# A two-layer decoder trunk on one Trainium2 core: product order, copy placement and stream splits around the Strassen stage and the first stick-breaking group

## The chip, the cores and the metric

One core of a Trainium2 chip. The metric is device time in microseconds of one execution, the median of several runs; lower is better. The engines are TensorE (PE), VectorE (DVE), ScalarE (ACT), GpSimd (POOL) and SyncE (SP), which here issues the DMAs.

## The reference, cut to what matters

512 tokens of width 2048 pass through two layers. Layer 0 is sparse attention with an indexer (top 128 keys of a query), layer 1 is stick-breaking attention over keys and values that are computed once from the stream. Each layer ends in a projection, a LayerNorm over `ALPHA * x + h`, and a gated per-layer embedding.

```python
def mixer_b(x, w_in, w_o, k, v):
    q, gate = jnp.split(x @ w_in, [WIDTH_B], axis=-1)
    ...
        z = jnp.einsum('bqngd,bsnd->bngqs', qg, k) * (HEAD_DIM ** -0.5)
        strict = key_pos[None, :] < t[:, None]
        log_om = jnp.where(strict, -jax.nn.softplus(z), 0.0)
        suffix = lax.cumsum(log_om, axis=log_om.ndim - 1, reverse=True) - log_om
        a = jnp.where(strict, jnp.exp(jax.nn.log_sigmoid(z) + suffix), 0.0)
        o = jnp.einsum('bngqs,bsnd->bqngd', a, v)
    ...
    return (o * jax.nn.silu(gate)) @ w_o

for i in range(DEPTH):                       # DEPTH = 2, layer 0 uses mixer_a
    h = mixer(x)
    x = layer_norm(ALPHA * x + h, ln_g[i], ln_b[i])
    x = x + (p[i] @ w_ple[i]) * jax.nn.sigmoid(x @ w_ple_gate[i])
```

16 heads of 128 in four groups that share keys and values; all arrays are float32.

## The kernel before, in words

**Precision.** Every float32 operand is split in two: `split` copies it to a rounded high part on ScalarE (`ACTIVATE`, line 111 in the profile, the common helper) and subtracts it on VectorE for the low part. `mm3` (lines 134 to 136) then makes a product of three matmuls: high by high, high by low, low by high. A product of a 128-row weight block with 512 columns is three matmuls of 512 columns.

**Weights.** They come through `next_raw`: 512 KB loads on SP's queue into three `raw` buffers, in the order of the list `units`, which also holds blocks of the stream `x` and, in layer 1, the two halves of `x2` that have to come back from DRAM. `plain_items` and `strassen_items` split them into `wh` and `wl` (three buffers each); `Ahead` keeps two blocks split ahead of the one in use.

**Order.** TensorE's order is the program's. On the other engines a planner may move an instruction forward when it is ready, unless it is pinned: `keep_in_program_order` sets it behind the instruction traced last on its engine (which may itself have been moved forward). `Paced` pins everything while `pinned[0]` is set. Small pieces of work wait in the queue `bg`; `pumped` issues one of them, pinned, after every n-th product, `drain` the rest. `interleave` spreads the products of one generator between the steps of another.

**Start.** `first_items` brings, for each pair k2 of 128-row blocks, a stream unit and two weight units (`iq` and `k`). It splits the stream blocks (`xh`, `xl`) and the weights.

**Strassen.** The value projection and the four query projections of layer 1 are five chunks of Strassen's method (Winograd's form) with seven products over 256 token columns. `gemm_s` runs k over eight steps of two weight blocks j, that is 14 products a step. `strassen_items` makes the weight sums `s1` to `s4` in `st` (four VectorE additions a step) and splits them into `sh` and `sl`. The seven sums build up in seven of the eight PSUM banks; `product_banks` shifts the banks by one from chunk to chunk, so that product i of a chunk uses the bank in which product i-1 of the chunk before was left. In `gemm_s`, the first step (k=0) fetches both weight blocks and issues products 0 to 2 of both and then 3 to 6 of both; all later steps go block by block. `combine` reads the banks into four quarters: three copies by ScalarE (`u`, `c21`, `c12`), two VectorE additions, three more in `rest`, and three `onto` additions that go to `bg`.

**Stick-breaking.** Four groups g of four heads, ten units u = (i, kb) each, by the generator `sticks`: `logits` (product `z`, then Abs, Exp, Ln on ScalarE, a VectorE operation, a GpSimd mask on the diagonal, and the split `sh`, `sl`), `weights` (two or four matmuls with triangular matrices onto `z`, Exp, split), `values` (product `o`). Between their steps stand the products of that group's gate projection (16 weight blocks of four products). For group 0, `gate_first` takes the blocks 8 to 15 first, since blocks 0 to 7 have to be restored: the right half of `xh` and `xl` held Strassen sums, and `restore` splits the returned halves of `x2` into them. `split_keys`, `split_scaled` and `split_values` make the split keys, scaled queries and values. The first 20 gate products of group 0 run alone, with those splits in `bg`; then `px`, a pool that holds the work tiles of the sticks, is opened where the value tiles were.

**Last part.** `finish_layer` does projection, LayerNorm and embedding, once a layer; it is not changed.

Of the kernel before, what the change touches and what calls it, by code (L numbers as in the profile page):

```python
# [18 lines left out]
T = 512  # L19
# [58 lines left out]
def trunk_kernel(  # L78
# [79 lines left out]
    def plain(kb):  # L158
        return XH[kb], XL[kb]
# [159 lines left out]
    bg = deque()  # L319

    def paced(fn, *args):
        pinned[0] = True
        fn(*args)
        pinned[0] = False

    def one():
        paced(bg.popleft())
# [8 lines left out]
    def drain():  # L336
        while bg:
            one()
# [42 lines left out]
    def gemm_s(items, C3, M):  # L381

        rows = M[0].shape[1]
        for k in range(NK // 2):
            b11, t1 = ((XH[k][:, s], XL[k][:, s]) for s in (slice(0, H), slice(H, T)))
            b21, b22 = ((XH[k + 8][:, s], XL[k + 8][:, s]) for s in (slice(0, H), slice(H, T)))
            t2, t3, t4 = ((C3[k][0][:, i], C3[k][1][:, i]) for i in range(3))
            sides = (b11, b21, t2, t3, t1, b22, t4)
            terms = []
            for j in range(rows):  # L390
                pinned[0] = k == j == 0
                a11, a22, a12, s1, s2, s3, s4 = next(items)
                pinned[0] = False
                terms.append((a11, a12, s2, s3, s1, s4, a22))
                if k:
                    order = [(i, j) for i in range(7)]
                elif j == rows - 1:

                    order = [(i, n) for some in (range(3), range(3, 7)) for n in range(rows) for i in some]
                else:  # L400
                    continue
                for i, n in order:
                    first, final = (n == 0, n == 1) if rows == 2 else (i % 2 == 0, i % 2 == 1 or i == 6)
                    mm3(M[i][:, n], terms[n][i], sides[i], k == 0 and first, k == NK // 2 - 1 and final)
                    yield

    def quarter(x, i, j0=0, rows=2):
# [5 lines left out]
    def combine(wp, M, dst):  # L413

        m1, m2, m6, m7, m5, m3, m4 = M
        u = wp.tile([128, 2, H], F32, name="u", tag="u", bufs=1)[:, : m1.shape[1]]
        c11, c22, c12, c21 = (dst(i) for i in range(4))
        pinned[0] = True
        act.activation(u, m1, AF.Copy)
        act.activation(c21, m7, AF.Copy)  # L420
        act.activation(c12, m5, AF.Copy)
        dve.tensor_tensor(c11, m2, u, ALU.add)
        dve.tensor_tensor(u, m6, u, ALU.add)
        pinned[0] = False
# [10 lines left out]
        return [lambda c=c: onto(c) for c in (c12, c21, c22)]  # L435

    def build_plain(k):
        for n in (k, k + 8):
# [76 lines left out]
    for g in range(4):  # L515
        add_job(w_in_b, g * 512, strassen=True)
    x2 = dram.tile([D, T], F32, name="x2")
    for k in (4, 5, 6, None, 7, None, 0, 1, 2, 3):
        if k is None:
            first = 4 * (units[-1][1] == 14)  # L520
# [590 lines left out]
    finish_layer(0, xT, x2, (pk_, pv_), first_sums, first_blocks)  # L1111


    with ps_:
        sp = ps_.enter_context(tc.tile_pool(name="sp1", bufs=1))
        C3.extend(c3_tiles(sp, range(4, 8)))
# [14 lines left out]
        for n, dst in enumerate((Vf, *F)):  # L1131
            M = product_banks(4 - n)
            gemm = pumped(gemm_s(items, C3, M), 8)
            if n == 1:
                steps(gemm, 40)
                for t in range(4):
                    steps(gemm, 16)
                    turn_values(t)
            run(gemm)
            drain()  # L1140
            bg.extend(combine(sp, M, lambda i: quarter(dst, i)))
        drain()

    pc_ = ExitStack()
    pc = pc_.enter_context(tc.tile_pool(name="pc", bufs=1))
# [7 lines left out]
    def split_values(t):  # L1153
        split(*V[t], Vf[:, :, t * 128 : (t + 1) * 128])

    def split_scaled(g, i):
        qh, ql = (pc.tile([128, 4, 128], F32R, name=f"q{s}", tag=f"q{s}", bufs=4) for s in "hl")
# [5 lines left out]
    def restore(raw, k):  # L1163
        split(XH[k][:, H:T], XL[k][:, H:T], raw[:, k % 4])

    def gate_items():
        for k, n in ((0, 6), (4, 2)):
            yield from plain_items([(512, n)])
            raw = next_raw()
            bg.extend(lambda raw=raw, k=k: restore(raw, k) for k in range(k, k + 4))  # L1170
        yield from plain_items([(512, 8), *[(512, NK)] * 3])

    items = Ahead(gate_items(), 2)

    def gate_first(banks):

# [14 lines left out]
    pv_.close()  # L1191
    px_ = ExitStack()
    px = px_.enter_context(ss(name="px", bufs=1, side="right"))

    def work():
        return px.tile([128, 512], F32, name="wk", tag="wk", bufs=4)
# [5 lines left out]
    def sticks(g, Q):  # L1202
# [34 lines left out]
        def weights(u):  # L1237
# [6 lines left out]
            act.activation(a, z, AF.Exp)  # L1244
            if kb == i:
                strict(a)
            parts = tuple(px.tile([128, 512], F32R, name=f"a{s}", tag=f"a{s}", bufs=2) for s in "hl")
            split(*parts, a)
            state[u] = parts

# [6 lines left out]
                act.activation(F[g][:, :, i * 128 : (i + 1) * 128], out[i].rearrange("p (h q) -> p h q", h=4), AF.Copy)  # L1257

        for s in range(12):
            for fn, u in ((logits, s), (weights, s - 1), (values, s - 2)):  # L1260
                if s == 1 and fn == weights:
                    for _ in range(4):
                        yield
                if 0 <= u < 10:
                    fn(u)
                    yield

    for g in range(4):
        tc.keep_in_program_order(act.preload_act_table_set("natural_log_exp_and_others"))
        if g:  # L1270
            banks = mm_banks("g")
            gemm = pumped(gemm_w(items, plain, banks))
        if g < 3:
            bg.append(lambda g=g: split_keys(g + 1))
        interleave(sticks(g, Q), 30 + 4, gemm, 52 if g else 40, lead=8 * (g > 0))
        if g < 3:
            for i in range(4):
                split_scaled(g + 1, i)
# [57 lines left out]
```

## Time and profile before

| | us |
|---|---|
| median of 3 runs | 1887.45 (1887.42 to 1887.73) |
| the profiled execution | 1888.32 |
| its span, first to last instruction | 1886.6 |
| TensorE busy | 1873.0 (99%) |
| VectorE busy | 1192.3 (63%) |
| ScalarE busy | 940.0 (50%) |
| Strassen chunks, from about | 1033.7 to 1242.5 |
| stick-breaking, first group, from about | 1242.5 to 1314 |

The granted TensorE clock is 1.00 throughout. DMAs take about a third of the 16 engines' time. In a timeline row stand the start, the duration, the engine, the line, the operation, what it writes and reads, and in brackets how long its engine was idle before it and what ended that; `sh` in Strassen is a weight sum, in the sticks a split of the softplus; `f` and `E` are result tiles.

### The profile page before, as it was taken

To read this page: it belongs to the slowest core of one execution; us is meant where nothing else is said; L and a number is where in the kernel's file an instruction comes from. 1 tells how busy PE (TensorE), PEld (TensorE's weight loads), DVE (VectorE), ACT (ScalarE), POOL (GpSimd) and SP (SyncE) were. 2 spreads that over 40 slices of the span, in tenths; PEclk is the share of its full clock that TensorE was granted. 3 is DMA by queue.
4 is the path that set the end of the run, shared out by engine and by line. 5 is a ranking of instruction groups with operands and counts; after the bars stand their busy time and mean duration, and the time that the engine had idled before them with its cause. 6 is when DMAs were issued, how large, how long until landed. Compare 5 with 4: busy or idle time off the path is not lost.

```text
span 1886.6 us, 25028 instructions
## 1 busy us (share of the span) xinstructions
PE 1873.0 (99%) x9229; PEld 1585.3 (84%) x9229; DVE 1192.3 (63%) x2327; ACT 940.0 (50%) x1714; POOL 26.4 (1%) x46
## 2 busy tenths in 40 slices
PE   9999999999999999999999999999999999999998
PEld 8898888888888888888888999987888888888887
DVE  4768678566555455675368878876655545567534
ACT  3546333456554432474245444468877743347422
POOL 0000000000000000000000000000100000000000
PEclk9999999999999999999999999999999999999999
DMA  5432333322222532423343333331122153242333
GB/s 184 137 115 65 101 91 100 97 60 68 68 68 67 178 101 73 128 91 112 115 139 112 101 102 101 101 112 56 56 67 68 59 187 99 74 129 89 123 101 112
DMA packets 111179, 189.22 MB, mean 100 GB/s; under 512 B 8528, under 2 KB 29008, under 8 KB 111056
## 3 DMA queue, kind: packets, MB, share of 16 engines
q1 hardware_dynamic: 111056, 187.62, 32.5%
q8 instruction: 72, 1.18, 0.3%
q14 instruction: 51, 0.42, 0.1%
HBM read 179.21 MB, written 8.39 MB: 99 GB/s over the span
## 4 chain that ended last, share of the span: by engine, by line
PE 94%; DVE 2%; ACT 1%; DMA 1%; issue 1%; SPq 0%; DVEq 0%; ACTq 0%
PE g L135 12%; PE g L134 12%; PE g L136 12%; PE o L135 7%; PE o L136 7%; PE o L134 7%; PE q L134 3%; PE q L135 3%; PE q L136 3%; PE m L136 3%; PE m L135 3%; PE m L134 3%; PE z L1242 2%; PE k L135 1%; PE k L136 1%; PE k L134 1%
## 5 line engine op out<-in xcount | busy, mean ns | idle before, releaser
L111 ACT ACTIVATE wh<-raw 128x512 fp32r<-128x512 f32 (+3 forms) x685 | 396.2, 580 | 653.0 <-PE g L135 231.9
L111 DVE TENSOR_TENSOR wl<-raw,wh 128x512 fp32r<-128x512 f32 (+3 forms) x685 | 429.4, 629 | 448.9 <-ACT wh L111 430.4
L134 PE MATMUL g<-xh,wh 128*128 128x512 f32 x1024 | 403.9, 394 | 0.2
L135 PE MATMUL g<-xl,wh 128*128 128x512 f32 x1024 | 400.6, 391 | 0.4 <-DVE xl L111 0.4
L136 PE MATMUL g<-xh,wl 128*128 128x512 f32 x1024 | 399.7, 390 | 0.0
L136 PEld LDWEIGHTS g<-xh,wl 128*128 128x128 f32 x1024 | 192.2, 188 | 41.0
L134 PEld LDWEIGHTS g<-xh,wh 128*128 128x128 f32 x1024 | 192.4, 188 | 39.5 <-ACT wk L111 1.1
L135 PEld LDWEIGHTS g<-xl,wh 128*128 128x128 f32 x1024 | 192.4, 188 | 38.8 <-DVE xl L111 1.2
L136 PE MATMUL o<-xh,wl 128*128 128x512 f32 x512 | 199.3, 389 | 0.0
L135 PE MATMUL o<-xl,wh 128*128 128x512 f32 x512 | 199.2, 389 | 0.0
L134 PE MATMUL o<-xh,wh 128*128 128x512 f32 x512 | 199.2, 389 | 0.0
L136 PEld LDWEIGHTS o<-xh,wl 128*128 128x128 f32 x512 | 96.1, 188 | 20.2 <-DVE wl L111 0.3
L135 PEld LDWEIGHTS o<-xl,wh 128*128 128x128 f32 x512 | 96.1, 188 | 20.1
L134 PEld LDWEIGHTS o<-xh,wh 128*128 128x128 f32 x512 | 96.1, 188 | 19.9
L134 PE MATMUL q<-xh,wh 128*128 128x512 f32 x256 | 99.6, 389 | 0.0
L135 PE MATMUL q<-xl,wh 128*128 128x512 f32 x256 | 99.6, 389 | 0.0
L136 PE MATMUL q<-xh,wl 128*128 128x512 f32 x256 | 99.6, 389 | 0.0
L111 ACT ACTIVATE sh<-st 128x512 fp32r<-128x512 f32 x80 | 49.5, 629 | 84.7 <-PE m L135 46.6
L111 DVE TENSOR_TENSOR sl<-st,sh 128x512 fp32r<-128x512 f32 x80 | 54.4, 689 | 41.1 <-ACT sh L111 41.1
L111 DVE TENSOR_TENSOR xl<-f,xh 128x512 fp32r<-128x512 f32 x80 | 54.3, 686 | 11.3 <-ACT f L111 11.0
L111 ACT ACTIVATE wk<-z 128x512 f32<-128x512 f32 x80 | 47.3, 591 | 25.1 <-PE z L136 17.2
L136 PEld LDWEIGHTS q<-xh,wl 128*128 128x128 f32 x256 | 48.1, 188 | 10.0
(286 smaller groups left out, 3345.1 us busy)
## 6 DMA issues: line engine op xcount, KB each, us to landing
raw<-w_in_a SPq DMA_DIRECT2D x95, 512.0 KB, 3.7
raw<-w_in_b SPq DMA_DIRECT2D x64, 512.0 KB, 3.8
raw<-w_ple_gate SPq DMA_DIRECT2D x52, 512.0 KB, 3.7
raw<-w_o_a SPq DMA_DIRECT2D x24, 512.0 KB, 3.7
raw<-w_o_b SPq DMA_DIRECT2D x24, 512.0 KB, 3.7
raw<-w_kv_b SPq DMA_DIRECT2D x16, 512.0 KB, 3.7
raw<-w_ple_gate SPq DMA_DIRECT2D x24, 256.0 KB, 2.9
f<-xT SPq DMA_DIRECT2D x4, 1024.0 KB, 6.5
```

Source lines behind the costliest of these rows:

```text
L111: ins = method(*args, **kw)
L134: pe.matmul(out, a[0], b[0], start=start, stop=False)
L135: pe.matmul(out, a[0], b[1], start=False, stop=False)
L136: pe.matmul(out, a[1], b[0], start=False, stop=stop)
L1242: pe.matmul(z, m, p, start=False, stop=n == len(terms), skip_group_check=True)
```

## The change

What it does, in the order of the diff:

- In `first_items`, the splits of stream blocks are pinned from k2 = 2 on, so they stand behind the weight splits traced before them.
- `paced` restores what `pinned[0]` was.
- `gemm_s` issues all seven products of a weight block before it fetches the next, in k=0 too.
- `combine` copies `m5` to `c22` instead of `c12`, and `rest` reads bank `m3` first. After the last chunk, `combine_last` takes its place: one ScalarE copy and seven VectorE additions, all pinned, nothing in `bg`. Ahead of it the first two gate blocks are split.
- The returned halves of `x2` come after the gate's units 4 to 7 and after unit 0; their restores follow in `bg` when the ninth and the eleventh gate block are fetched, with the queries of i = 3 and the keys of group 1 behind them.
- In group 0 the ScalarE table for Exp and Ln is loaded right after the last chunk. Only the keys and two query blocks are split first; nine gate products, the first logits, one gate product, the second logits, eight gate products beside which two value blocks are split, the first weights, two more gate products with the other value blocks. The rest, 44 gate products, is spread over 27 steps (before: 44 left after the lead of 20, 40 of them over 34 steps), with one piece of `bg` after every second product.
- The work pool `px` lies apart from the values now; only the split weights (`ah`, `al`) go where the values were, and the first unit's use query buffers.
- Of the next group's four query splits, three go to `bg` during the group; before, all four came at its end.

```diff
@@ first_items
-            if k2:
-                for a in range(2):
-                    split(*plain(2 * k2 + a), x[:, a])
+            for n in (2 * k2, 2 * k2 + 1) if k2 else ():
+                was, pinned[0] = pinned[0], k2 > 1
+                split(*plain(n), x[:, n % 2])
+                pinned[0] = was
@@ gemm_s
-                terms.append((a11, a12, s2, s3, s1, s4, a22))
-                if k:
-                    order = [(i, j) for i in range(7)]
-                elif j == rows - 1:
-                    order = [(i, n) for some in (range(3), range(3, 7)) for n in range(rows) for i in some]
-                else:
-                    continue
-                for i, n in order:
...
+                terms = ((a11, b11), (a12, b21), (s2, t2), (s3, t3), (s1, t1), (s4, b22), (a22, t4))
+                for i, (a, b) in enumerate(terms):
...
@@ combine
-        act.activation(c12, m5, AF.Copy)
+        act.activation(c22, m5, AF.Copy)
...
-            dve.tensor_tensor(c22, c12, c21, ALU.add)
-            dve.tensor_tensor(c12, m3, c12, ALU.add)
+            dve.tensor_tensor(c12, m3, c22, ALU.add)
+            dve.tensor_tensor(c22, c22, c21, ALU.add)
             dve.tensor_tensor(c21, c21, m4, ALU.subtract)
...
+    def combine_last(wp, M, dst):
...
+        act.activation(u, m1, AF.Copy)
+        for out, a, b, op in (
+            (c11, m2, u, ALU.add),
+            (u, m6, u, ALU.add),
+            (c21, m7, u, ALU.add),
+            (c22, m5, c21, ALU.add),
+            (c12, m5, u, ALU.add),
+            (c12, m3, c12, ALU.add),
+            (c21, c21, m4, ALU.subtract),
+        ):
+            dve.tensor_tensor(out, a, b, op)
@@ units
-    for k in (4, 5, 6, None, 7, None, 0, 1, 2, 3):
+    for k in (4, 5, 6, 7, None, 0, None, 1, 2, 3):
@@ gate_items
-        for k, n in ((0, 6), (4, 2)):
+        for k, n in ((0, 8), (4, 2)):
             yield from plain_items([(512, n)])
             raw = next_raw()
             bg.extend(lambda raw=raw, k=k: restore(raw, k) for k in range(k, k + 4))
+            bg.append((lambda: split_scaled(0, 3)) if k == 0 else (lambda: split_keys(1)))
-        yield from plain_items([(512, 8), *[(512, NK)] * 3])
+        yield from plain_items([(512, 6), *[(512, NK)] * 3])
@@ group 0
-    bg.append(lambda: split_keys(0))
-    for i in range(4):
-        bg.append(lambda i=i: split_scaled(0, i))
-        bg.append(lambda i=i: split_values(i))
-    banks = mm_banks("g")
-    gemm = pumped(gate_first(banks))
-    steps(gemm, 20)
+    log_exp()
+    bg.append(lambda: split_keys(0))
+    bg.extend(lambda i=i: split_scaled(0, i) for i in range(2))
+    banks = mm_banks("g")
+    chunk = gate_first(banks)
+    gemm = pumped(chunk)
+    steps(gemm, 9)
+    first = sticks(0, Q)
+    steps(first, 1)
+    steps(gemm, 1)
+    steps(first, 1)
+    bg.extend(lambda i=i: split_values(i) for i in range(2))
+    steps(gemm, 8)
+    drain()
+    steps(first, 1)
+    bg.extend(lambda i=i: split_values(i) for i in range(2, 4))
+    steps(gemm, 2)
...
+    bg.append(lambda: split_scaled(0, 2))
+    gemm = pumped(chunk, 2)
...
-        interleave(sticks(g, Q), 30 + 4, gemm, 52 if g else 40, lead=8 * (g > 0))
+        if g:
+            interleave(sticks(g, Q), 30 + 4, gemm, 52, lead=8)
+        else:
+            interleave(first, 30 - 3, gemm, 64 - 20)
```

More of the change, by code (lines that the diff above doesn't have):

```diff
@@ L321, in paced @@
     def paced(fn, *args):
-        pinned[0] = True
+        was, pinned[0] = pinned[0], True
         fn(*args)
-        pinned[0] = False
+        pinned[0] = was
     def one():
@@ L435, in combine @@
         return [lambda c=c: onto(c) for c in (c12, c21, c22)]
+    def combine_last(wp, M, dst):
+        m1, m2, m6, m7, m5, m3, m4 = M
+        u = wp.tile([128, 2, H], F32, name="u", tag="u", bufs=1)
+        c11, c22, c12, c21 = (dst(i) for i in range(4))
+        pinned[0] = True
+        act.activation(u, m1, AF.Copy)
[9 more added lines that the diff above has]
+            dve.tensor_tensor(out, a, b, op)
+        pinned[0] = False
     def build_plain(k):
@@ L517, in trunk_kernel @@
     x2 = dram.tile([D, T], F32, name="x2")
-    for k in (4, 5, 6, None, 7, None, 0, 1, 2, 3):
+    for k in (4, 5, 6, 7, None, 0, None, 1, 2, 3):
         if k is None:
-            first = 4 * (units[-1][1] == 14)
+            first = 4 * (units[-1][1] == 0)
             units.append((x2.rearrange("(k p) t -> p k t", p=128)[:, first : first + 4, H:T],))
@@ L1111, in trunk_kernel, with restore, gate_items @@
     finish_layer(0, xT, x2, (pk_, pv_), first_sums, first_blocks)
+    def restore(raw, k):
+        split(XH[k][:, H:T], XL[k][:, H:T], raw[:, k % 4])
+    def gate_items():
+        for k, n in ((0, 8), (4, 2)):
+            yield from plain_items([(512, n)])
+            raw = next_raw()
+            bg.extend(lambda raw=raw, k=k: restore(raw, k) for k in range(k, k + 4))
+            bg.append((lambda: split_scaled(0, 3)) if k == 0 else (lambda: split_keys(1)))
+        yield from plain_items([(512, 6), *[(512, NK)] * 3])
     with ps_:
@@ L1140, in trunk_kernel @@
             drain()
-            bg.extend(combine(sp, M, lambda i: quarter(dst, i)))
-        drain()
+            if n == 4:
+                items = Ahead(gate_items(), 2).prime()
+                combine_last(sp, M, lambda i: quarter(dst, i))
+            else:
+                bg.extend(combine(sp, M, lambda i: quarter(dst, i)))
     pc_ = ExitStack()
@@ L1246, in weights @@
                 strict(a)
-            parts = tuple(px.tile([128, 512], F32R, name=f"a{s}", tag=f"a{s}", bufs=2) for s in "hl")
+            if u or g:
+                parts = tuple(pa_late[0].tile([128, 512], F32R, name=f"a{s}", tag=f"a{s}", bufs=2) for s in "hl")
+            else:
+                parts = [a.rearrange("p h q -> p (h q)") for a in scaled_parts()]
             split(*parts, a)
@@ L1259, in sticks @@
         for s in range(12):
+            if s > 2 and units[s - 3][1] == 0 and g < 3:
+                bg.append(lambda i=units[s - 3][0]: split_scaled(g + 1, i))
             for fn, u in ((logits, s), (weights, s - 1), (values, s - 2)):
-                if s == 1 and fn == weights:
-                    for _ in range(4):
-                        yield
                 if 0 <= u < 10:
@@ L1266, in sticks @@
                     yield
+                if g and s == 1 and fn == logits:
+                    for _ in range(4):
+                        yield
+    log_exp()
[15 more added lines that the diff above has]
+    steps(gemm, 2)
+    pv_.close()
+    pa_late.append(px_.enter_context(ss(name="pal", bufs=1, side="right")))
+    bg.append(lambda: split_scaled(0, 2))
+    gemm = pumped(chunk, 2)
     for g in range(4):
-        tc.keep_in_program_order(act.preload_act_table_set("natural_log_exp_and_others"))
         if g:
+            log_exp()
             banks = mm_banks("g")
             gemm = pumped(gemm_w(items, plain, banks))
-        if g < 3:
-            bg.append(lambda g=g: split_keys(g + 1))
-        interleave(sticks(g, Q), 30 + 4, gemm, 52 if g else 40, lead=8 * (g > 0))
-        if g < 3:
-            for i in range(4):
-                split_scaled(g + 1, i)
+        if 0 < g < 3:
+            bg.append(lambda g=g: split_keys(g + 1))
+        if g:
+            interleave(sticks(g, Q), 30 + 4, gemm, 52, lead=8)
+        else:
+            interleave(first, 30 - 3, gemm, 64 - 20)
+        drain()
+        if g < 3:
+            split_scaled(g + 1, 3)
         for h in range(4):
```

23 lines of the change are left out of this document (9 added, 14 removed).

## The prediction, as put on record before the run

> **What bounds the kernel now.** I read the page first, then the waits of TensorE (PE), then the timeline around each wait. In the page, busy time by engine:
>
> ```profile
> span 1886.6 us, 25028 instructions
> ...
> PE 1873.0 (99%) x9229; PEld 1585.3 (84%) x9229; DVE 1192.3 (63%) x2327; ACT 940.0 (50%) x1714; POOL 26.4 (1%) x46
> ```
>
> TensorE is idle for 13.6 us of the span. No matmul is added or removed by the change, so it can only win back stalls of TensorE or make new ones. Who ended those stalls is in the view of waits (us in total, times, longest):
>
> ```profile
> PE m L136 <- DVE sl L111: 2.2, 4, 0.6
> PE z L1242 <- ACT sh L111: 1.4, 2, 0.9
> PE spun L156 <- DVE xl L111: 1.4, 1, 1.4
> PE m L136 <- DVE wl L111: 1.2, 4, 0.3
> PE z L1242 <- DVE sl L111: 0.8, 3, 0.3
> PE iq L134 <- ACT wh L111: 0.6, 1, 0.6
> ```
>
> Three places: the Strassen products `m` (3.4 us idle in eight waits), the first stick-breaking group `z` (2.2 in five), one stall in the first projection `iq`. The diff touches all three. Idle time understates a stall, since a matmul's row overlaps its successor; I count lost time between starts.
>
> **Strassen's boundary.** The TensorE timeline where the third of five chunks begins:
>
> ```profile
> 1117.46 0.28 PE L134 MATMUL m<-xh,wh 128*128 128x256 f32 x1
> ...
> 1122.62 0.28 PE L135 MATMUL m<-xl,wh 128*128 128x256 f32 x1
> 1123.12 0.39 PE L136 MATMUL m<-xh,wl 128*128 128x256 f32 x1 [0.21 <-DVE wl L111]
> ...
> 1123.91 0.28 PE L135 MATMUL m<-c3l,sh 128*128 128x256 f32 x1
> 1124.66 0.39 PE L136 MATMUL m<-c3h,sl 128*128 128x256 f32 x1 [0.48 <-DVE sl L111]
> ```
>
> The chunk starts at 1117.46. Its k=0 is 14 products of three matmuls, 42 starts; 1122.62 is the 44th start after it, so a matmul takes 5.16 / 43 = 0.12 and a product 0.36. Then 1122.62 to 1123.12 should be 0.12 and is 0.50, and 1123.91 to 1124.66 is 0.75: lost 0.38 + 0.63 = 1.01 for 0.69 idle. Scaled to the 3.4 idle of the eight waits: 3.4 x 1.01 / 0.69 = 5.0 us over four boundaries. What VectorE does meanwhile:
>
> ```profile
> 1118.05 0.68 DVE L111 TENSOR_TENSOR u<-m,u 128x512 f32<-128x512 f32 x1
> 1118.65 0.68 DVE L111 TENSOR_TENSOR f<-f 128x512 f32<-128x512 f32 x1
> 1119.43 0.69 DVE L111 TENSOR_TENSOR f<-m,f 128x512 f32<-128x512 f32 x1
> 1120.04 0.68 DVE L111 TENSOR_TENSOR f<-f,m 128x512 f32<-128x512 f32 x1
> 1120.64 0.42 DVE L111 TENSOR_TENSOR st<-st,raw 128x256 f32<-128x256 f32 x1
> 1120.97 1.29 DVE L111 TENSOR_TENSOR f<-f,u 128x512 f32<-128x512 f32 x2
> 1122.18 0.42 DVE L111 TENSOR_TENSOR st<-raw,st 128x256 f32<-128x256 f32 x1
> 1122.51 1.49 DVE L111 TENSOR_TENSOR wl<-raw,wh 128x384 fp32r<-128x384 f32 x3
> 1123.92 1.89 DVE L111 TENSOR_TENSOR sl<-st,sh 128x512 fp32r<-128x512 f32 x3
> ```
>
> These are the previous chunk's sums (`u`, three of `rest`), then `s2` of the next weight block, two `onto` additions, only then `s4`, and the copies `wl` and `sl` that TensorE waits for. Before the change both blocks of k=0 are fetched ahead of any product, so an `onto` is pinned only behind the second block's last instruction, which the planner had already floated forward; so two slip in between `s2` and `s4`.
>
> After it, the first block's `s2`, `s4`, `wl`, `sl` are traced, then one product, then the first `onto`, pinned behind that `sl`. The second `onto` can still slip. Step by step: the three `rest` operations stay three, `s2` at 1120.64; `s4` right behind it (1121.0) or behind one `onto` of 0.6 (1121.6); `wl` (1.41 / 3 = 0.47 each) done by 1121.5 to 1122.5; `sh` on ScalarE and then `sl` (0.6 each) done by 1122.6 to 1123.3. TensorE wants `wl` at 1122.74 and `sl` at 1117.46 + 14 x 0.36 + 2 x 0.36 + 0.24 = 1123.46. Both are in time, with 0.2 to spare in the worse case. The `onto`s and the second block come after; it is wanted 2.52 later, and has about 1.9 of VectorE's work ahead of it. So the 5.0 us go.
>
> What is late next is a PSUM bank. Plain order reaches product 4 after 3 products, not 6: at 1117.46 + 1.08 = 1118.54. That bank held `m6`, and its reader `u<-m,u` ends at 1118.73. A wait of 0.19 and some 0.06 of signal: 0.25, four times 1.0 us; bounds 0 (VectorE does it one 0.33 `st` earlier) and 2.0 (one 0.47 copy gets in front, less the slack). The seventh product is at 1119.62; its bank's reader now comes right behind `u`, at 1118.65 + 0.68 = 1119.33, which is why the swap in `rest` matters: left at 1119.43 + 0.69 = 1120.12 it would cost 0.5 each. Net for Strassen: -4.0 (between -5.0 and -3.0).
>
> `combine_last` issues seven VectorE additions and one ScalarE copy for eight and three. The fourth gate bank was emptied by ScalarE and is now emptied by the third VectorE operation; at a boundary's pace it would be free 1.27 + 0.60 = 1.87 after the chunk's end, and is wanted after three gate products of three matmuls of 0.23, 2.04. Nothing lost: the cover is 0.17 at that pace, and if it goes, the cost is that excess, once.
>
> **The first stick group.** TensorE, then ScalarE, GpSimd (POOL), and the table of stretches (length, busy PE, PEld, DVE, ACT, POOL, clock, DMA share, GB/s):
>
> ```profile
> 1262.03 0.39 PE L136 MATMUL g<-xh,wl 128*128 128x512 f32 x1
> 1263.33 0.50 PE L1242 MATMUL z<-sh,tri 128*128 128x512 f32 x1 [0.92 <-ACT sh L111]
> 1264.06 0.50 PE L1242 MATMUL z<-sl,tri 128*128 128x512 f32 x1 [0.23 <-DVE sl L111]
> ```
>
> ```profile
> 1253.92 1.32 ACT L111 ACTIVATE xh<-raw 128x256 fp32r<-128x256 f32 x4
> 1255.26 1.28 ACT L111 ACT_TABLE_LOAD   x1
> ```
>
> ```profile
> 1242.50:1256.10 13.60, 13.60 (x62) 11.27 (x61) 13.44 (x25) 9.91 (x20) 0.00 (x0) 1.00 0.29 83
> 1256.10:1285.00 28.90, 26.67 (x110) 20.13 (x109) 20.07 (x35) 25.92 (x51) 4.20 (x6) 1.00 0.35 108
> ```
>
> A 512-column matmul is 0.23, so 1262.03 to 1263.33 lost 1.07 and the next step 0.50: 1.57 for 1.15 idle. Scaled to 2.2 idle: 3.0 us. The cause is ScalarE, busy 25.92 of 28.90 in the group's first half, and only 9.91 of 13.60 before. The change takes from that half the table load (1.28), the first restored half (1.32), and the chains of the first two logits, and puts them into the emptier stretch or behind.
>
> Now z(0) comes after 9 gate products instead of 20, and weights(0) after gate, z(1) and 8 gate products: 10 x 0.68 = 6.8 after z(0) ends. Before, it was 1 gate, z(1) and 6 gates: 8 x 0.68 = 5.4, and 1.07 late; so 6.5 sufficed even with everything in the way. The later units gain too: 44 gate products now fill 27 steps (1.63 each) where 40 filled 34 (1.18); over four gaps that is 4 x 0.45 x 0.68 = 1.2 us more between a logits and its weights, against waits of at most 0.9. I keep 0.5 as residue, because for some 8 us from weights(0) on ScalarE has values, queries, two weight blocks and restores of 0.3 to 0.6 each in front of two logits. Bounds: 0 and all 3.0. Net -2.5.
>
> What is queued behind the moved steps: the seven pinned sums stand on VectorE ahead of `kl` and `ql`. They end about 4.5 us into the gate, z(0) wants them at 9 x 0.68 = 6.1; two copies of 0.6 fit. On SP's queue the halves of `x2` go behind four weight units; each holds one of three `raw` buffers for 8 gate products. The weight load that waits for it is wanted 9 gate products later, over 6 us, longer where sticks lie between. The restores come 8 gate products (5.4 us) ahead of their first reader, at one restore for every two products. Next groups' queries go one by one into gaps of the old group: same work, no price.
>
> A row speaks against more copies around the diagonal masks:
>
> ```profile
> 1269.81 0.64 POOL L1200 TENSOR_SCALAR_AFFINE_SELECT wk<-wk 128x512 f32<-128x512 f32 x1 [3.84 <-ACT wk L111]
> 1274.74 1.02 POOL L1200 TENSOR_SCALAR_AFFINE_SELECT run<-run 128x512 f32<-128x512 f32 x1 [4.30 <-DVE run L111]
> ```
>
> A select takes 0.64, once 1.02; four lie on logits chains of the group, so 4 x 0.38 = 1.5 is the most this adds to the chains, and the spacing above absorbs it for three. The Trainium skill's "SBUF — State Buffer", section "Who interferes with whom", says that a VectorE instruction with two SBUF inputs and a GpSimd instruction that reads SBUF exclude each other for the whole instruction; by that rule the delay could reach a whole copy, 4 x 0.68 = 2.7, and the group's gain would be 0.3 instead of 2.5. The trace shows 0.38 at the worst select, so I stay with the rows.
>
> **The start.**
>
> ```profile
> 26.48 1.15 ACT L111 ACTIVATE xh<-raw 128x512 fp32r<-128x512 f32 x2 [5.67 <-DMA raw<-xT]
> 27.54 1.65 ACT L111 ACTIVATE wh<-raw 128x512 fp32r<-128x512 f32 x3
> ```
>
> ```profile
> 27.29 0.34 PE L136 MATMUL iq<-xh,wl 128*128 128x384 f32 x1
> 28.20 0.44 PE L134 MATMUL iq<-xh,wh 128*128 128x384 f32 x1 [0.57 <-ACT wh L111]
> 28.48 0.33 PE L135 MATMUL iq<-xl,wh 128*128 128x384 f32 x1
> 29.09 0.45 PE L136 MATMUL iq<-xh,wl 128*128 128x384 f32 x1 [0.28 <-DVE wl L111]
> ```
>
> ScalarE stood 5.67 us before a block of the stream that was still on its way, with a ready weight block behind it. At 0.17 a matmul, 0.74 + 0.44 = 1.2 are lost. Pinned, the stream's splits (k2 from 2) stand behind the weights of the pair before; a pair is about 11 us of matmuls, and the split waits for about a quarter of it, so it still comes several us early. Gain -1.2, bounds 0 and -1.2.
>
> **The sum.** -4.0 - 2.5 - 1.2 = -7.7; two small gaps at the group switches, whose four query copies are now mostly made earlier, may give 0.5 more, of which I take 0.2. -7.9 on the profiled execution's 1888.32 is 1880.4. The median of the three runs is 1887.45, 0.87 below it; there: **1879.6 us**.
>
> **Rivals.** *The copies keep slipping.* VectorE's order is the planner's choice wherever nothing is pinned; the second `onto` and copies of later blocks may still go before `s4`, and the bank wait comes on top. Two slips of 0.6 leave `sl` about 0.5 late, with the bank wait 0.75 of 1.25 kept at each boundary. Strassen then gives 2.0, all together 5.9: 1881.6; with the group's residue at 2 as well, 1883.1. For it: `s4` behind two `onto`s today. Against: the first is now pinned.
>
> *It doesn't do what it says.* What is unpinned floats back to where it was, or each stall gets a successor of its size: 1887.5, 0 to 2 either way.
>
> *Slower: ScalarE bounds the first group.* Today it is 90% busy over half of the group. If the pinned pieces put it behind, TensorE's in-order queue stands at each of ten weights, not five times. At 1.57 a wait that is 15.7, less the 3.0 already there: +12.7, with -4.0 and -1.2 elsewhere +7.5: 1895. It decides when the chain of a unit exceeds the 6.7 us of TensorE's work between a logits and its weights. Against it: the old need of 6.5.
>
> **The numbers.** Forecast 62%, slipping copies 18%, no effect 10%, slower 10%. About 0.2%, 3.8 us, is what a measurement can tell from no change, so faster (below 1883.7) 0.80, same 0.10, slower 0.10. All stalls gone and no bank wait would be 5.0 + 3.0 + 1.2 + 0.5 = 9.7, 1877.7; scaling idle to lost time may be short by a tenth: low end 1876.7. High end: slipping copies and a residue, 1884.0; beyond it lie the last two cases.
>
> **What would show it.** In the waits: no `m <- sl` or `m <- wl`, instead `m <- DVE u` of 0.1 to 0.3 four times; `z <- sh` gone or under 0.5; no `iq` wait near 28. In VectorE's timeline `s4`, `wl`, `sl` ahead of the first `onto`. The table load at about 1241, and ACT's share in the group's first half well under 90%. I am wrong if `m` waits on `f` or still on `sl`, or if the `z` waits grow in number.

## The result, and the profile after

| | before | after |
|---|---|---|
| median, us (lowest to highest of six runs each, same chip) | 1887.52 (1887.41 to 1887.88) | 1880.09 (1879.05 to 1881.19) |
| ratio to before | | 0.9961, interval 0.9948 to 0.9974 |
| the profiled execution, its span | 1888.32, 1886.6 | 1879.05, 1877.2 |

The forecast was 1879.6, range 1876.7 to 1884.0. From the page of the kernel after, span and busy time by engine:

```profile
span 1877.2 us, 25016 instructions
...
PE 1868.1 (100%) x9229; PEld 1586.2 (85%) x9229; DVE 1192.1 (64%) x2326; ACT 939.2 (50%) x1712; POOL 26.5 (1%) x46
```

Span minus busy PE was 13.6 and is 9.1. The span fell by twice that, 9.4, because lost starts and slower matmuls count as busy. TensorE's waits after (total, times, longest):

```profile
PE spun L156 <- DVE xl L111: 1.4, 1, 1.4
PE z L134 <- ACT qh L111: 1.0, 1, 1.0
PE z L1255 <- ACT sh L111: 0.5, 1, 0.5
PE z L135 <- DVE ql L111: 0.4, 1, 0.4
PE g L135 <- DVE xl L111: 0.4, 2, 0.2
PE z L1255 <- DVE sl L111: 0.2, 1, 0.2
```

All eight `m` waits and both `iq` waits are gone from this table; of `z` two smaller ones stay, and waits for `qh` and `ql` are new. To size every loss alike, *lost time* below is the sum, over a stretch, of each matmul's start-to-start time less the median for its shape in the kernel before:

| kernel | start | Strassen | group 0 | groups 1 to 3 | rest | span |
|---|---|---|---|---|---|---|
| before | 1.98 | 5.42 | 4.82 | 3.77 | 9.29 | 1886.6 |
| after | 0.44 | 1.85 | 3.59 | 1.44 | 8.51 | 1877.2 |
| start alone | 0.44 | 5.39 | 4.81 | 3.78 | 8.83 | 1884.6 |
| Strassen alone | 1.54 | 1.84 | 5.30 | 3.76 | 9.19 | 1883.0 |
| sticks alone | 1.90 | 5.40 | 3.62 | 1.46 | 8.80 | 1882.5 |
| after, fourth query first | 0.44 | 1.83 | 2.02 | 2.58 | 9.09 | 1877.3 |
| after, run again | 0.44 | 1.83 | 5.42 | 1.41 | 9.06 | 1879.5 |
| after, old `rest` | 0.44 | 2.83 | 5.36 | 1.42 | 9.50 | 1880.9 |
| before, 32 bytes | 2.25 | 5.37 | 4.41 | 3.82 | 8.68 | 1885.9 |
| before, 96 bytes | 1.94 | 5.41 | 3.92 | 1.15 | 7.35 | 1881.1 |
| after, 32 bytes | 0.44 | 1.80 | 3.82 | 2.23 | 8.14 | 1877.8 |
| after, 96 bytes | 0.44 | 1.84 | 3.53 | 0.74 | 7.52 | 1875.4 |
| combined | 0.44 | 3.43 | 1.29 | 0.72 | 7.68 | 1874.9 |
| 96 bytes and query first | 0.44 | 1.87 | 1.29 | 0.71 | 7.28 | 1872.9 |

(Groups 1 to 3 are the last three stick groups; "rest" is the first 60 matmuls, the middle and the last part.) From before to after the rows give 1.54 + 3.57 + 1.23 + 2.33 + 0.78 = 9.45, the 9.4 of the spans. Two entries are surprises: group 0 gave half of what was forecast, and groups 1 to 3, for which 0.2 was forecast, gave 2.33. The rows below the second belong to the experiments.

**Strassen's boundary after.** TensorE, then VectorE, at the third chunk (the chunk starts at 1114.31):

```profile
1115.27 0.28 PE L136 MATMUL m<-c3h,sl 128*128 128x256 f32 x1
...
1115.63 0.39 PE L134 MATMUL m<-c3h,sh 128*128 128x256 f32 x1
1115.86 0.28 PE L135 MATMUL m<-c3l,sh 128*128 128x256 f32 x1
```

```profile
1114.89 0.68 DVE L111 TENSOR_TENSOR u<-m,u 128x512 f32<-128x512 f32 x1
1115.50 0.68 DVE L111 TENSOR_TENSOR f<-m,f 128x512 f32<-128x512 f32 x1
...
1117.61 0.42 DVE L111 TENSOR_TENSOR st<-st,raw 128x256 f32<-128x256 f32 x1
1117.95 0.68 DVE L111 TENSOR_TENSOR f<-f,u 128x512 f32<-128x512 f32 x1
1118.55 0.42 DVE L111 TENSOR_TENSOR st<-raw,st 128x256 f32<-128x256 f32 x1
1118.88 1.02 DVE L111 TENSOR_TENSOR wl<-raw,wh 128x384 fp32r<-128x384 f32 x2
1119.82 0.68 DVE L111 TENSOR_TENSOR sl<-st,sh 128x512 fp32r<-128x512 f32 x1
1120.42 0.69 DVE L111 TENSOR_TENSOR f<-f,u 128x512 f32<-128x512 f32 x1
```

The fourth product starts at 1115.63, 0.24 late, as its bank is read by `u<-m,u` until 1115.57: the bank wait of the forecast, 0.20 to 0.24 at the four boundaries, with another 0.10 in the step behind it. One `onto` (1117.95) did get between `s2` and `s4`, the worse of the two cases that the prediction allowed; the second now comes after `sl` (1120.42) and not before it.

At the other three boundaries `sl` is still late, by waits too short for the table. VectorE, then TensorE, at the second chunk:

```profile
1077.44 0.69 DVE L111 TENSOR_TENSOR sl<-st,sh 128x512 fp32r<-128x512 f32 x1
```

```profile
1077.95 0.28 PE L135 MATMUL m<-c3l,sh 128*128 128x256 f32 x1
1078.19 0.39 PE L136 MATMUL m<-c3h,sl 128*128 128x256 f32 x1
```

The second matmul starts 0.24 after the first instead of 0.12, and the next step loses another 0.10. So a boundary loses 0.34 in all at the third chunk and 0.51 to 0.52 at the others, where 0.25 was forecast.

**Group 0 after.** TensorE and ScalarE around the new wait:

```profile
1275.80 0.50 PE L134 MATMUL z<-qh,kh 128*128 128x512 f32 x1 [1.01 <-ACT qh L111]
1276.69 0.50 PE L135 MATMUL z<-ql,kh 128*128 128x512 f32 x1 [0.39 <-DVE ql L111]
```

```profile
1267.99 0.63 ACT L111 ACTIVATE wh<-raw 128x512 fp32r<-128x512 f32 x1 [1.02 <-DMA raw<-w_in_b]
1268.53 0.40 ACT L111 ACTIVATE xh<-raw 128x256 fp32r<-128x256 f32 x1
...
1272.33 0.71 ACT L111 ACTIVATE xh<-raw 128x256 fp32r<-128x256 f32 x2
...
1275.13 0.61 ACT L111 ACTIVATE qh<-f 128x512 fp32r<-128x512 f32 x1
```

The logits of the fourth query block lose 1.17 + 0.67 = 1.84: its split was put into `bg` behind four restored blocks (`xh`), and ScalarE also stood 1.02 for a weight load. Two stretches of the lengths used in the prediction, laid from the start of the gate, and one from z(0), which now starts at 1242.79 (length, busy PE, PEld, DVE, ACT, POOL):

```profile
1236.65:1250.25 13.60, 13.60 (x62) 11.27 (x61) 10.58 (x17) 8.93 (x16) 1.27 (x2) 1.00 0.36 106
1250.25:1279.15 28.90, 26.75 (x114) 20.82 (x113) 21.70 (x37) 25.25 (x51) 2.92 (x4) 1.00 0.26 78
1242.79:1271.69 28.90, 28.15 (x123) 22.61 (x122) 21.42 (x35) 25.01 (x48) 4.19 (x6) 1.00 0.23 73
```

ScalarE hardly got lighter where it mattered: 25.25 of 28.90, or 25.01 from z(0) on, before 25.92.

### The profile page after: what moved, and what is told of

The parts are those of the page before. It is cut to its first block, busy times and chain, and to the rows that moved or that the text cites. A ratio compares the mean times of both kernels' runs of the same rounds, so it can differ in the third digit from the quotient of the medians.

```text
span 1877.2 us, 25016 instructions
## 1 busy us (share of the span) xinstructions
PE 1868.1 (100%) x9229; PEld 1586.2 (85%) x9229; DVE 1192.1 (64%) x2326; ACT 939.2 (50%) x1712; POOL 26.5 (1%) x46
## 3 DMA queue, kind: packets, MB, share of 16 engines
q8 instruction: 72, 1.18, 0.3%
## 5 line engine op out<-in xcount | busy, mean ns | idle before, releaser
L134 PEld LDWEIGHTS q<-xh,wh 128*128 128x128 f32 x256 | 48.0, 188 | 10.1
```

Source lines behind the costliest of these rows:

```text
L134: pe.matmul(out, a[0], b[0], start=start, stop=False)
```

## The experiments

In the comparisons the kernel before took 1887.97 (first four), 1887.95 (next four), 1887.84 (next three) and 1887.28 (last).

**The three parts, each alone on the kernel before.**

```diff
 e1: before, with in first_items
+                was, pinned[0] = pinned[0], k2 > 1
+                split(*plain(n), x[:, n % 2])
 e2: before, with gemm_s and combine of the change
 e3: the change, with first_items, gemm_s and combine of before
```

> The kernel before with the stream splits pinned, nothing else. Theory (the three parts act apart, each through its own stalls of TensorE): the two iq waits near 28 us go, 1.2 to 2.0 us less than before, about 1886.0. Rival (the pinned splits only move the wait to the next stream load): within 0.4 of 1887.5.

1886.35 (1885.94 to 1886.95), ratio 0.9992 (0.9983 to 1.0): 1.6 less, at the edge of what can be told. No `iq` wait is left, and start loses 0.44.

> The kernel before with plain product order, the copy of m5 in c22 and bank m3 read first; combine after the last chunk as before. Theory: m waits on sl and wl go, a bank wait of about 0.2 lost comes at each of four boundaries, 3.5 to 4.5 us less than before, about 1883.5. Rival (the gain of the changed kernel lies in the sticks, Strassen's copies still slip): under 2 us less, about 1886.

1884.70, ratio 0.9983 (0.9974 to 0.9992): 3.3 less, a little under the 3.5 to 4.5 expected. The `m` waits go, but the first group takes some back; its first wait grows from 0.9 to 1.4, since TensorE gets there earlier and ScalarE doesn't:

```profile
PE z L1233 <- ACT sh L111: 1.9, 2, 1.4
```

> The changed kernel with the old product order, the old combine and unpinned stream splits: the change around the first stick group and combine_last alone. Theory: 2 to 3.5 us less than before, about 1885, with m waits on sl and wl of before's size and the iq waits near 28. Rival (ScalarE bounds the group and the new waits there eat the gain): no gain, 1887 or more.

1884.89, ratio 0.9985 (0.9976 to 0.9994): 3.1 less, 1.2 of lost time in group 0 and 2.3 in groups 1 to 3. The three sum to 8.0, the whole change gave 7.4 to 7.9 (1880.09 and, run again, 1880.10): the parts add up.

**The fourth query first**, to see whether `bg`'s order makes the new wait.

```diff
+            if k == 0:
+                bg.append(lambda: split_scaled(0, 3))
             bg.extend(lambda raw=raw, k=k: restore(raw, k) for k in range(k, k + 4))
-            bg.append((lambda: split_scaled(0, 3)) if k == 0 else (lambda: split_keys(1)))
+            if k:
+                bg.append(lambda: split_keys(1))
...
-            if s > 2 and units[s - 3][1] == 0 and g < 3:
+            if g and s > 2 and units[s - 3][1] == 0 and g < 3:
                 bg.append(lambda i=units[s - 3][0]: split_scaled(g + 1, i))
+            if g == 0 and s > 8:
+                bg.append(lambda i=s - 9: split_scaled(1, i))
```

> The changed kernel with the fourth query split put ahead of the first four restores, and the next group's queries in group 0 not before step 9. Theory (bg's order makes the sixth logits wait 1.8 us for its query and the third weights 1.2 for ScalarE): both mostly gone, 1.5 to 3 us less than the changed kernel, about 1878. Rival (ScalarE is held by a weight block whose load comes late, the order in bg matters little): 1879.5 to 1880.5.

1879.21 (1879.05 to 1879.69), ratio 0.9954 (0.9941 to 0.9966). The `qh` and `ql` waits are gone and group 0 loses 2.02 instead of 3.59. But the next group's queries, put late by the second half of the edit, now meet the switch, where a new wait stands:

```profile
PE g L134 <- ACT wk L111: 0.6, 1, 0.6
```

The traced spans are nearly equal (1877.3 and 1877.2): of the 1.57 that group 0 gained, groups 1 to 3 took 1.14 and "rest" 0.58, and the expected 1878 was not reached.

The waits at the weights of the third unit (0.68 and 0.50 lost, for `sh` and `sl`) did not move. This doesn't clear the query copy that stands ahead of them: in the changed kernel it is the next group's (`qh`, 1257.67 to 1258.29), and in this run the fourth query's stands in the same place. ScalarE is without a pause from 1253.03 until it makes the `sh` at 1259.15, with copies of values, queries and a weight block between the steps of the logits. Which of them costs the 1.18 was not tested.

**The change again.**

> The changed kernel itself, beside the next three. Both theories expect 1879 to 1881 us, as at its first measurement, and the same waits: product 4 waits 0.20 to 0.24 at four chunk boundaries, weights(2) loses 0.68 and 0.50, logits(6) 1.17 and 0.67.

1880.10 (1879.79 to 1881.39). The traced execution was the slowest, and shows why they spread:

```profile
1276.52 0.51 PE L134 MATMUL z<-qh,kh 128*128 128x512 f32 x1 [1.27 <-ACT qh L111]
...
1278.35 0.63 PE L135 MATMUL g<-xl,wh 128*128 128x512 f32 x1
1278.78 0.63 PE L136 MATMUL g<-xh,wl 128*128 128x512 f32 x1
```

```profile
1278.00:1281.50 3.50, 3.50 (x10) 2.73 (x9) 1.37 (x3) 2.68 (x5) 0.00 (x0) 0.51 0.03 13
```

Behind the `qh` wait, matmuls start every 0.43 instead of 0.23, and the granted clock (after the five engines) is 0.51 for 3.5 us: 1.6 us on top of the wait.

**The old `rest`**, all else as changed.

```diff
-        act.activation(c22, m5, AF.Copy)
+        act.activation(c12, m5, AF.Copy)
...
-            dve.tensor_tensor(c12, m3, c22, ALU.add)
-            dve.tensor_tensor(c22, c22, c21, ALU.add)
+            dve.tensor_tensor(c22, c12, c21, ALU.add)
+            dve.tensor_tensor(c12, m3, c12, ALU.add)
```

> The changed kernel with the old combine: m5 copied to c12, and rest in the old order (c22 from c12 and c21 first, then m3). My step: the bank of m3 is then free only about 1120.12 in the old timeline where the seventh product is wanted at 1119.62, so a wait of 0.5 us appears at each of the four boundaries that a combine precedes, ahead of the seventh product, 2.0 us slower than the changed kernel. Rival: the wait for product 4 already shifts everything after it by 0.2 and VectorE is ahead by then, so 4 x 0.2 or nothing.

1882.06 (1880.30 to 1882.91), ratio 0.9968 (0.9955 to 0.998). The wait at the seventh product appears:

```profile
1159.24 0.39 PE L134 MATMUL m<-c3h,wh 128*128 128x256 f32 x1 [0.20 <-DVE f L111]
```

It loses 0.22 to 0.36 at the four boundaries, each with 0.10 behind it, 1.7 in all where my 0.5 each gave 2.0. Strassen loses 2.83 instead of 1.83, only 1.0 more: TensorE comes later to `sl`, and the 0.7 lost there at three boundaries is gone. The rest of the difference between the medians fits the half-clock stretch: by their clock three of its five executions had it, and two of the five of the changed kernel.

**Where do groups 1 to 3 get 2.3 us?** No wait there explains it. The view of groups by shape shows shorter matmuls (duration in ns: least, median, most), of the kernel before and after:

```profile
L1242 PE MATMUL z<-sh,neg x12: 397/397/398, 1271.3 to 1491.0; 128*128 128x512 f32 x12
L134 PE MATMUL o<-ah,vh x40: 392/396/398, 1268.2 to 1504.2; 128*128 128x512 f32 x40
```

```profile
L1255 PE MATMUL z<-sh,neg x12: 389/389/389, 1258.7 to 1481.7; 128*128 128x512 f32 x12
L134 PE MATMUL o<-ah,vh x39: 397/397/398, 1262.3 to 1494.8; 128*128 128x512 f32 x39
```

`z<-sh,neg` streams `sh` from `px`, which the change moved; `o<-ah,vh` streams `ah`, which stayed on the right side of SBUF. From start to start the first fell from 236 to 227 ns, the second is 236. In the compiled programs' tables of addresses, the streamed tiles of the left side lie on multiples of 128 bytes, those of the right side 96 bytes past one (the profile holds no addresses, so the traces show shifts of a tile, not these remainders). A tile that nobody uses, reserved at the right end, moves the whole right side:

```diff
+    ctx.enter_context(tc.tile_pool(name="pad", bufs=1, side="right")).tile([128, 8], F32, name="pad")
```

> The kernel before with one tile of 32 bytes per partition reserved at the right end of SBUF, never read or written; nothing else differs. All tiles of the right side move down by 32 bytes: px, sh and ah among them from an address that leaves 32 when divided by 64 to a multiple of 64; px stays on the right. Theory A (the address modulo 64 of the streamed operand sets the pitch, and the gain of groups 1 to 3 came from moving px): z<-sh,tri falls from 236 to 227 ns, o<-ah,vh too (which the change left at 236), groups 1 to 3 lose about 1.4 us instead of 3.8 and less than that for o, and the other matmuls that stream from the right side (first layer's s<-kh,qh 236, sum<-th 235, pe<-ptl 238) fall as well: 2.5 to 4.5 us faster than before. Theory B (what counts is which side px lies on, or who else writes near it): pitches stay, time within 0.5 us of before. Theory C (the gain came from the new order of the groups' work, not from the place): as B.

1887.36, ratio 0.9997 (0.9988 to 1.0006). The work of the four compute engines stands in the order of the kernel before. Theory A in this form, multiples of 64, fell: `sh` lay on one and cost as much as before:

```profile
L1243 PE MATMUL z<-sh,neg x12: 395/397/398, 1270.9 to 1490.7; 128*128 128x512 f32 x12
```

Some rows of other stages did fall, from start to start `s<-kh,qh` from 236 to 228 ns and `pe<-ptl,wh` from 237 to 229.

> The changed kernel with the same 32 bytes reserved: px is already at a multiple of 64, so only ah and al of pal and the right-side tiles of the other stages move onto one. Theory A: z stays at 227, o<-ah,vh falls from 236 to 227 (117 matmuls by 6 to 9 ns, 0.9 us), with first-layer and final-stage rows 1.5 to 2.5 us faster than the changed kernel in all, some 1877 to 1878. Theories B and C: no difference, 1879 to 1881.

1879.66 (1879.57 to 1879.91), ratio 0.9958 (0.9945 to 0.997): `ah` stays at 237 ns, and there is no gain beyond the spread of the changed kernel. But 32 bytes had left the right side 64 past a multiple of 128. With 24 elements instead of 8 it gets onto one:

> The kernel before with 96 bytes per partition reserved at the right end, where the run with 32 left z<-sh,tri at 236 ns. Addresses modulo 128 of the right side: 96 in the kernel before, 64 with a pad of 32, 0 here; every operand of the left side, px as the change places it among them, has 0. Theory A2 (a streamed operand off a multiple of 128 costs, on itself and the few matmuls behind it): z<-sh,tri and o<-ah,vh at 227, s<-kh,qh from 236 to 227, groups 1 to 3 lose 3.8 - 3.0 = 0.8 us, the middle of the kernel 5.3 - 1.5; 3.5 to 5 us faster than before, 1883 to 1884.5. Theory B (the side of SBUF counts, or the order of the work in the groups): pitches stay and so does the time, 1887 to 1888.

1882.98 (1882.53 to 1883.84), ratio 0.9974 (0.9965 to 0.9984): 4.9 less, from 96 unused bytes.

```profile
L1243 PE MATMUL z<-sh,neg x12: 388/390/390, 1269.8 to 1486.6; 128*128 128x512 f32 x12
L135 PE MATMUL o<-ah,vh x40: 388/389/397, 1266.7 to 1499.5; 128*128 128x512 f32 x40
```

`px` is on the right, its old place, the work of the four compute engines stands in the old order, and groups 1 to 3 lose 1.15 instead of 3.77. So the address is enough to make the gain. It is not every row: `s<-kh,qh` of the first layer, forecast to fall to 227, stays at 236 from start to start, though 32 bytes brought it to 228. A multiple of 128 is therefore not the whole rule, and that stays open.

> The changed kernel with the same 96 bytes reserved. Theory A2: o<-ah,vh from 236 to 227 and the matmuls behind it too (groups 1 to 3 lose 1.4 - 1.0), the first layer's and last stage's rows as well, 2 to 3 us faster than the changed kernel, 1877 to 1878. Theory B: 1879.6 to 1880.1, pitches unchanged.

1879.24 (1877.29 to 1879.47), ratio 0.9952 (0.994 to 0.9965). The traced execution, at 1877.29, lost 0.74 in groups 1 to 3, where 0.4 was expected; the median misses the 1877 to 1878, as the other four executions were 1.5 to 2.2 us slower, three of them at a lower mean clock. No trace shows these four, so the cause is only argued: the size is that of the half-clock stretch, and the `qh` wait was 1.28 here.

**Combined**, with the fourth query first (the next group's queries left where the change has them) and one more edit against the bank wait: the product with `s1` goes ahead of the one with `s3`.

```diff
-                for i, (a, b) in enumerate(terms):
+                for i in (0, 1, 2, 4, 3, 5, 6) if k == j == 0 and rows == 2 else range(7):
+                    a, b = terms[i]
```

> The changed kernel with the 96 bytes, with product 4 taken before product 3 in the first block of a chunk, and with the fourth query split of the first group put ahead of the four restores of the first half (next group's queries stay as the change has them). Product 4 one place later is wanted 0.36 us later, which covers the wait of 0.20 to 0.24 at four boundaries: Strassen loses 1.0 instead of 1.85; product 3's bank, now earlier by nothing and used one place sooner, may cost at most the 0.36 it moves back. The query split first: the wait of 1.0 to 1.27 for qh and 0.39 for ql goes (-1.8 us of lost time, and the half-clock stretch of 1.5 us behind it in some executions). With theory A2's 2 to 3 us: 1874 to 1876; by theory B 1877 to 1878. If the next group's queries at their early place meet the fourth split, a wait of 0.3 to 0.7 comes at the switch to group 1 as in the run with the query first and the next queries late.

(There, "product 4 before product 3" counts from zero, and the waiting "product 4" counts from one, as in the prediction.) 1876.65 (1876.42 to 1877.31), ratio 0.9942 (0.9929 to 0.9956). Group 0 loses 1.29 and no new wait came at the switch, but Strassen loses 3.43 instead of 1.84. The bank wait is gone, and with it came another:

```profile
PE m L137 <- DVE sl L111: 0.7, 3, 0.2
```

At the third chunk, where the copies keep their order, `sl` alone now comes 0.25 late, with 0.10 behind it: the bank wait had covered this. At the other three TensorE also releases a weight buffer earlier; ScalarE now makes `wh` 5.12 us after the chunk's start and `sh` only at 5.55, where the changed kernel makes `sh` at 4.86, and VectorE a third `wl` ahead of `sl`. A boundary lost 0.34 at the third chunk and 0.51 to 0.52 elsewhere; it now loses 0.34 and 1.03 to 1.05.

**The two that helped, without that.**

> The combined kernel without the exchange of products 3 and 4, so: the changed kernel, the 96 bytes, and the fourth query split of the first group ahead of the first four restores. If the exchange was what cost 3.4 instead of 1.8 us at the chunk boundaries (it has TensorE ask for sl one product earlier than VectorE has it), those waits go back to 0.20 to 0.24 at product 4, and the rest stays as in the combined kernel: 1876.65 - 1.6 = 1875.0 us, the first group losing 1.2 to 1.3, groups 1 to 3 0.7. Rival: the exchange had nothing to do with it and the boundary's copies are late because the query split or the 96 bytes changed the planner's order; then Strassen stays at 3.4 and the time at 1876.6.

1874.96 (1874.83 to 1875.34), ratio 0.9935 (0.9922 to 0.9949); Strassen is back at 1.87. This beats both kernels. Its waits on TensorE, all that the table of waits has:

```profile
PE spun L157 <- DVE xl L111: 1.4, 1, 1.4
PE z L1259 <- ACT sh L111: 0.5, 1, 0.5
PE g L136 <- DVE xl L111: 0.5, 2, 0.2
PE z L1259 <- DVE sl L111: 0.2, 1, 0.2
```

## Why the prediction was right, and where only by chance

- **The sum.** -7.9 was forecast, -7.4 measured, 9.3 between the traced executions: that of before was 0.8 above its median, that of after, the fastest of six, 1.0 below. The terms of the start and of Strassen held; those of the sticks were 1.3 too large and 2.1 too small. The sum is right partly by that, and so by luck; the traced pair also won 0.78 in "rest", for which no term stood.
- **The start, -1.2.** Right in mechanism, 1.6 alone, 1.54 of lost time: two smaller losses behind the two counted steps went as well.
- **Strassen, -4.0.** 3.57 of lost time, 3.3 alone. The long waits went: they had cost 5.4, not 5.0. The bank wait came where and as large as forecast (0.20 to 0.24; forecast 0.25), with 0.10 on the next step not counted. The swap in `rest` is worth 1.0, not 2.0, as the waits that it avoids would cover those for `sl`. The rival of slipping copies was half true: one `onto` slipped, and "0.2 to spare" was not there. `sl` is wanted 6.00 after the chunk's start (1123.46 less 1117.46) and was to be done by 5.84 at the worst; it is done at 6.20 to 6.37. The bank wait, which holds TensorE back by 0.30 to 0.34, covers this at one boundary and all but 0.12 to 0.13 at three. The combined run, without the bank wait, shows it.
- **Group 0, -2.5: the failed step is the residue.** 0.5 was kept of 3.0; 1.18 remains at the weights of the third unit, and 1.84 is new at the fourth query's logits. What misled me is a sentence on ScalarE: "The change takes from that half the table load (1.28), the first restored half (1.32)". Their rows are at 1253.92 and 1255.26, ahead of z(0) at 1256.1, so but for 0.44 of the table load they were never in the half whose 25.92 I read. Into the stretch of 25.25 came the four value splits, and seven of the eight restores where four had stood. I checked the slack of the weights and not the place of the fourth query in `bg`, although the diff shows it behind four restores. "ACT's share in the group's first half well under 90%" was the sign, and 25.25 of 28.90 is 87%. The rival in which ScalarE bounds the group did not come: two units of ten wait.
- **Groups 1 to 3, -0.2: an effect that I did not see.** 2.33: 0.9 on the `z` products themselves and 1.5 on the gate products between them. The 96 bytes give 0.9 and 1.3 on the same rows with the old order of work, so most of it is `px`'s address, though no run moves `px` alone. The prediction has no term for the line of the diff that moves it. The rows of before held the clue: `z<-sh` took longer than `z<-qh` of the same shape.
- **The signs.** No `m <- sl` or `wl`, no `iq`: right by the table of waits, but by the starts `sl` is still waited for at three boundaries, which the prediction named as a sign of being wrong. The bank waits are too short for the table of waits, and show in starts only. `s4` behind the first `onto`, not ahead. The table load came at 1235.34, not about 1241, since ScalarE was free right after the last chunk's copy.
- **The rule on the shared port** (the Trainium skill's "SBUF — State Buffer", "Who interferes with whom"), by which group 0 would gain 0.3 (3.0 less 2.7; with the residue of 0.5 it would be a loss of 0.2): the gain was 1.2, but 1.84 of what is left is queue order on ScalarE, which the run with the query first undid without touching a mask. No run here tests the rule.

## What to carry to other kernels

When a matmul of one shape takes different times on different tiles, look at the tiles' addresses before the order of the work: 96 unused bytes gave 4.9 us here, more than any part of the change alone. When work is put into a queue of small pieces, list what stands ahead of each piece with its consumer's time; moving one query copy past four restores took 1.6 to 2.2 us of lost time and most of the spread between executions. And a wait that covers the late copies behind it is not free to remove.

## What the runs showed of the hardware

**Streamed operands.** With the right side's tiles in their place, 96 bytes past a multiple of 128 by the tables of addresses, the matmuls of the sticks and of the last part that stream 512 float32 columns from them mostly start every 231 to 237 ns, and some gate products between them are slowed too. A shift of 32 bytes leaves `z<-sh` and `o<-ah` at 232 to 237, but brings `pe<-ptl` from 237 to 229; a shift of 96, onto a multiple of 128, brings all of these to 227. Whether 128 is the modulus or all operands have to agree in a larger one is open (by the same tables all fast tiles also lay 128 past a multiple of 256), and so is why `s<-kh,qh` is fast at 32 and not at 96.

**The clock.** It fell to 0.51 for 3.5 us after waits of 1.27 (the change again) and 1.21 us (old `rest`), each with 0.39 behind it, but not after 1.01, 1.06, 1.28 or 1.42 us in other traces, so length alone doesn't decide. In all fourteen traces the changes of the granted clock lie a whole number of 3.41 us after the first. Laid on that grid, the change run again, and then Strassen alone with its wait of 1.42:

```profile
1274.62:1278.03 3.41, 1.76 (x7) 0.91 (x6) 2.42 (x4) 1.82 (x4) 0.00 (x0) 1.00 0.79 235
1278.03:1281.45 3.42, 3.42 (x10) 2.65 (x9) 1.32 (x3) 2.68 (x5) 0.00 (x0) 0.50 0.03 12
```

```profile
1256.57:1259.98 3.41, 1.99 (x9) 1.29 (x7) 1.99 (x5) 2.92 (x7) 0.64 (x1) 1.00 0.24 91
```

TensorE was idle for 1.65 of the 3.41 us ahead of the slow stretch here, and for 1.60 in the old `rest`; no other such window of the fourteen traces (from the first change of the clock on, the last 8 us of each left aside) has more than 1.42, and none is followed by half the clock. So it is the idle share of a window that goes with the drop in these runs, and where the grid falls makes the same kernel take either time: the wait of 1.28 lay across two windows, with 0.93 and 0.74 idle. The Trainium skill's "TensorE: Matmul & The Clock Gate", "Part 1", describes a free-running window of 3413 ns, with which these traces agree; its advice in "Why this matters for your kernels", no idle gaps over some 3 us, is too generous here by these rows.
